# Attention scores from 64-row half heads in place of zero-padded queries, in both blocks

## The chip, the cores and the metric

The kernel runs on one core of a Trainium2 chip. The metric is the device time of one execution in microseconds; the median of the runs shown stands for a kernel. The profile is of one further execution.

## What is computed

Two transformer blocks follow each other on 256 tokens of width 1024, all in float32. Of the first block, what matters here is neighbourhood attention with 8 heads of 64:

```python
proj = jnp.einsum('bsd,de->bse', h, w_in[l])
q, k, v, a, g = jnp.split(proj, splits, axis=-1)
...
s = jnp.einsum('brcqhd,brckwhd->bhrcqkw', qg, kg,
               preferred_element_type=jnp.float32) * (Dh ** -0.5)
s = s + bias.astype(jnp.float32)[None]
s = jnp.where(col_mask[:, :, None, :], s, -jnp.inf)
p = jax.nn.softmax(s, axis=(-2, -1))
```

A convolution branch, an output projection and an expert layer (16 experts, width 2048) follow. The second block has differential attention: 16 score heads of 64 form 8 pairs, and the softmax of the second of a pair, times lambda, is taken from that of the first. There are 256 queries and 512 keys (256 of a context, 256 of the tokens); queries and keys are rotated (rope).

```python
q = axial_rope(q, rows, cols)
k = axial_rope(k, rows, cols)
...
s = jnp.einsum('bqhd,bkhd->bhqk', qblk, k).astype(jnp.float32) * (DIFF_DH ** -0.5)
a = jax.nn.softmax(s, axis=-1).reshape(B, DIFF_HEADS, 2, Q_BLK, Lk)
a = a[:, :, 0] - lam * a[:, :, 1]
```

After it come a gating branch, output projections, and a retrieval layer that gathers 16 rows for each token and each of 8 heads from a table in memory.

## The kernel before

Queries and keys lie transposed: the 128 partitions of a chunk hold the 64 features of one head and, below them, the 64 of the next, and tokens run along the free axis. A score product of one head would have 64 rows only. The kernel before makes it a product of 128 rows instead. It keeps the queries twice as wide, with an axis for the half: in half 0 the lower 64 partitions are zeros, in half 1 the upper ones. Both products of a chunk then read the whole key chunk, and the zeros take the other head out.

Block 1. The buffer is `qz` (L346), cleared by POOL (L347). `q_evac` (L386) copies the projected queries from PSUM with two ScalarE instructions per pair of chunks, one for each half. `head_pair` (L424) has one chunk: for both halves `hh` and both blocks of 128 queries `t` it multiplies (L430) into one PSUM bank for each half; then come bias and maximum on VectorE (L434, L436), exponentials and scaling on ScalarE, transposes (L452) and the product with the values (L461). The latter writes the two heads to the two halves of the partitions and so has the 128*64 form. Four such generators are advanced by hand, among the value projection (`proj_N`, L111), the convolution (VectorE L366, and TensorE L376 for the last chunk) and the matrix products of the modulation (`ada`, L270, 128*32 form).

Block 2. The buffer is `q2z` (L862), in the slot of a weight buffer; POOL clears the two unused quarters (L863, L864). `blk_T` projects (L93). `rope_evac` (L874) copies a chunk to `rr` on ScalarE (L879), shuffles it (L880), multiplies by sine on POOL (L881) and by cosine on VectorE (L882), and adds on VectorE (L884): for queries in two adds of 64 partitions, one for each half, for keys in one add of 128. `attend` (L896) is a generator for chunk `d` and query block `t`, 16 in all: two products (L901) into two PSUM banks, softmax on VectorE and ScalarE (L905 to L912), transposes (L916), copy (L918), product with the values (L922). The loop at L947 advances them in turn with `fill`, which holds the other projections of the block (L111, L93).

A projection takes its weights in two parts: ScalarE rounds (`wh`, L68), VectorE, or POOL for every fourth part in block 2, subtracts (`wl`, L75). Weights are loaded on SP's queue into a ring of buffers. The order of the instructions on an engine is in most of the program not that of the text: a planner lays it out when the program is built, by what is ready, with the text's order as priority; only behind L1061 is it held to the text. In the profile, for instance, some products of L376 stand between those of L270 and the transposes L279 that the text has right behind L270.

In the profile a float32 product shows as two records of weight load and two of product.

Of the kernel before, what the change touches and what calls it, by code (L numbers as in the profile page):

```python
# [5 lines left out]
F32 = mybir.dt.float32  # L6
# [3 lines left out]
AF = mybir.ActivationFunctionType  # L10
# [26 lines left out]
def body(tc, A, out, x1_in=None, dump=None, parts="1234"):  # L37
    nc = tc.nc
    mm = nc.tensor.matmul
    tt_ = nc.vector.tensor_tensor  # L40
    act = nc.scalar.activation
# [77 lines left out]
    def run(g):  # L119
        for _ in g:  # L120
            pass
# [103 lines left out]
    W = w_es.enter_context(pool(name="W", bufs=1, side="right"))  # L225
# [99 lines left out]
    if "1" in parts:  # L325
        p1 = ExitStack()
        P1 = p1.enter_context(pool(name="P1", bufs=1))
# [5 lines left out]
        hl = HP.tile([128, 2, 8, 256], F32R, name="h0", tag="h")  # L333
# [8 lines left out]
        def sl(c2):  # L342
            return slice(c2 * 2, c2 * 2 + 2)


        qz = P1.tile([128, 4, 2, 256], F32, name="qz", tag="qz")  # L346
        nc.gpsimd.memset(qz, 0.0)  # L347
        kT = P1.tile([128, 4, 256], F32, name="kT")
        vv = P1.tile([128, 2, 512], F32, name="vv")
        mp = [P1]  # L350
# [33 lines left out]
            next(cv)  # L384
        next(ad)
        def q_evac(c2, p):  # L386
            for hh in range(2):
                r = slice(hh * 64, hh * 64 + 64)
                act(qz[r, sl(c2), hh], p[r], AF.Copy)

        for _ in proj_T(P1, wload(A["w_in"][0]), hl, q_evac):
            pass
# [31 lines left out]
        def head_pair(hc):  # L424

            sp = []
            for hh in range(2):
                p = ps((128, 2, 256))
                for t in range(2):
                    mm(p[:, 1 - t], lhsT=qz[:, hc, hh, t * 128:(t + 1) * 128], rhs=kT[:, hc, :], start=True, stop=True)  # L430
                s = P1.tile([128, 2, 256], F32, name="s", tag="of", bufs=6)
                b = bias[:, hc * 2 + hh]
                b = bass.AP(tensor=b.tensor, offset=b.offset, ap=[b.ap[0], [128, 2], [1, 256]])
                nc.vector.scalar_tensor_tensor(out=s, in0=p, scalar=0.125, in1=b, op0=OP.mult, op1=OP.add)  # L434
                st = P1.tile([128, 6], F32, name="st", tag="st", bufs=4)
                nc.vector.tensor_reduce(out=st[:, 0:2], in_=s, axis=AX.X, op=OP.max, negate=True)  # L436
                sp.append((s, st))
            yield
            for s, st in sp:
                for t in range(2):  # L440
                    act(s[:, t], s[:, t], AF.Exp, bias=st[:, t:t + 1], accum_out=st[:, 2 + t:3 + t])
                nc.vector.reciprocal(out=st[:, 4:6], in_=st[:, 2:4])
            for s, st in sp:
                for t in range(2):
                    act(s[:, t], s[:, t], AF.Copy, scale=st[:, 4 + t:5 + t])
            yield
            at = []
            for s, st in sp:
                pt = pq((128, 2, 256))
                for kc in range(2):  # L450
                    for t in range(2):
                        nc.tensor.transpose(pt[:, kc, t * 128:(t + 1) * 128], s[:, 1 - t, kc * 128:(kc + 1) * 128], ident)  # L452
                aT = P1.tile([128, 2, 256], F32, name="aT", tag="of", bufs=6)
                act(aT, pt, AF.Copy)
                at.append(aT)
            yield
            po = pq((128, 256), name="po")
            for kc in range(2):
                for hh in range(2):
                    h = hc * 2 + hh  # L460
                    mm(po[hh * 64:hh * 64 + 64, :], lhsT=vv[:, kc, h * 64:(h + 1) * 64], rhs=at[hh][:, kc], start=kc == 0, stop=kc == 1)  # L461
            act(oT[:, hc], po, AF.Copy)
            yield
# [395 lines left out]
    nc.scalar.dma_start(out=x_dr, in_=X.rearrange("p t d -> p (t d)"))  # L859
    ga = XP.tile([128, 8, 256], F32, name="ga", tag="x")  # L860
    ring[:2] = [0, 3]
    qz = W.tile([128, 8, 2, 256], F32, name="q2z", tag="wa", bufs=1)  # L862
    nc.gpsimd.memset(qz[0:64, :, 1], 0.0)  # L863
    nc.gpsimd.memset(qz[64:128, :, 0], 0.0)  # L864
    zg2 = W.tile([128, 2, 8, 256], F32, name="zg2", tag="wb", bufs=1)
    zu, gs = zg2[:, 0], zg2[:, 1]

    def blk_T(src, x, evac):
        return proj_T(P3, wload(src), x, evac, pool_every=4)
# [4 lines left out]
    def rope_evac(dst_of):  # L874
        def f(c2, p):
            for c in range(2):
                raw = AT.tile([128, 256], F32, name="rr", tag="rr", bufs=2)
                sh = AT.tile([128, 256], F32, name="rs", tag="rs", bufs=2)
                act(raw, p[:, c], AF.Copy)  # L879
                nc.vector.stream_shuffle(sh, raw, [i ^ 16 for i in range(32)])  # L880
                nc.gpsimd.tensor_tensor(out=sh, in0=sh, in1=rope[:, 1], op=OP.mult)  # L881
                tt_(out=raw, in0=raw, in1=rope[:, 0], op=OP.mult)  # L882
                for r, d in dst_of(c2 * 2 + c):
                    tt_(out=d, in0=raw[r], in1=sh[r], op=OP.add)  # L884
        return f

    for b in range(2):
        run(blk_T(WI[b], hl, rope_evac(lambda c: [(slice(i * 64, i * 64 + 64), qz[i * 64:i * 64 + 64, b * 4 + c, i]) for i in range(2)])))
    for b in range(2):
        run(blk_T(WI[2 + b], hl, rope_evac(lambda c: [(slice(0, 128), kall[:, b * 4 + c, 256:512])])))  # L890
    for b in range(2):
# [4 lines left out]
    def attend(d, t):  # L896

        st = AT.tile([128, 8], F32, name="ast", tag="ast", bufs=3)
        pp = [ps(name="psc") for _ in range(2)]
        for i in range(2):  # L900
            mm(pp[i], lhsT=qz[:, d, i, t * 128:(t + 1) * 128], rhs=kall[:, d, :], start=True, stop=True)  # L901
        yield
        e = [None, None]
        for i in range(2):
            nc.vector.tensor_reduce(out=st[:, i:i + 1], in_=pp[i], axis=AX.X, op=OP.max)  # L905
            nc.vector.tensor_scalar(out=st[:, i:i + 1], in0=st[:, i:i + 1], scalar1=-0.125, scalar2=None, op0=OP.mult)
            e[i] = AT.tile([128, 512], F32, name="e%d" % i, tag="e%d" % i, bufs=2)
            act(e[i], pp[i], AF.Exp, bias=st[:, i:i + 1], scale=0.125, accum_out=st[:, 2 + i:3 + i])
        nc.vector.reciprocal(out=st[:, 4:6], in_=st[:, 2:4])
        tt_(out=st[:, 6:7], in0=st[:, 5:6], in1=lam, op=OP.mult)  # L910
        nc.vector.tensor_scalar(out=e[1], in0=e[1], scalar1=st[:, 6:7], scalar2=None, op0=OP.mult)
        nc.vector.scalar_tensor_tensor(out=e[0], in0=e[0], scalar=st[:, 4:5], in1=e[1], op0=OP.mult, op1=OP.subtract)  # L912
        yield
        pt = ps((128, 4, 128))
        for kc in range(4):
            nc.tensor.transpose(pt[:, kc], e[0][:, kc * 128:(kc + 1) * 128], ident)  # L916
        aT = AT.tile([128, 4, 128], F32, name="a2T", tag="a2T", bufs=2)
        act(aT, pt, AF.Copy)  # L918
        yield
        po = ps((128, 128))  # L920
        for kc in range(4):
            mm(po, lhsT=aT[:, kc], rhs=vall[:, kc, d * 128:(d + 1) * 128], start=kc == 0, stop=kc == 3)  # L922
        nc.vector.tensor_copy(out=oall[:, t, d * 128:(d + 1) * 128], in_=po)
        yield
# [591 lines left out]
```

## Time and profile before

| | |
|---|---|
| three runs | 2153.0, 2155.0, 2160.1 us |
| median | 2155.0 us |
| profiled execution, its own time | 2150.8 us |
| its span | 2148.1 us |
| TensorE busy | 1647.5 us (77%) |
| VectorE busy | 907.8 us (42%) |
| ScalarE busy | 494.0 us (23%) |
| POOL busy | 461.2 us (21%) |

By time: block 1 up to about 165 us, the experts to about 1130, block 2's projections to 1215, its attention to 1330, the rest of its mixing to about 1450, and the gathers up to the end. Busy shares of the whole span mix stages with different limits; each stage is read by itself. TensorE's clock has two levels, 2.4 GHz (granted share 1.00) and 1.2 GHz (0.50); a share between is a mean over a stretch. Records of products overlap in time, since each holds its own ending; the distance of their starts, not their length, is what one costs in a row of them.

### The profile page before, as it was taken

The page shows a single profiled execution, that of the slowest core. Times are in us where ns is not written, and L with a number is a line of the kernel's source. Part 1 is how long each engine was busy: PE and PEld are TensorE (multiplying, and loading weights), DVE is VectorE, ACT ScalarE, POOL GpSimd, SP SyncE. Part 2 cuts the span into 40 slices and gives each one's busy share as a digit, 9 for nine tenths or more (in the row PEclk, how much of TensorE's full clock was granted, in tenths as well). Part 3 has the DMA queues.
Part 4 walks back from the last instruction along what each step waited for, and adds up shares of the span by engine and source line. Part 5 has one row for each costly group of instructions (what it writes and reads, how often), then busy time and mean ns, then how long its engine had stood idle before and what let it go on. Part 6 is the DMA issues. An engine that isn't in the chain of part 4 may idle for free. (4 is left out here: it accounts for less than half of the span.)

```text
span 2148.1 us, 21498 instructions
## 1 busy us (share of the span) xinstructions
PE 1647.5 (77%) x8132; PEld 850.3 (40%) x8132; DVE 907.8 (42%) x1951; ACT 494.0 (23%) x985; POOL 461.2 (21%) x341
## 2 busy tenths in 40 slices
PE   7998758776766566666567999985987887888776
PEld 7754213321211111111117889975443433443332
DVE  5833110000000000000008866856977766776754
ACT  5652100000000000000005556542222222232121
POOL 0012000000000000000003311224555555554552
PEclk9998887888878888778879999996999999999999
DMA  8779999999999999999995523528999999999996
GB/s 359 286 275 373 427 425 420 420 428 422 416 428 425 428 427 426 427 426 427 428 425 197 186 90 126 208 89 323 406 420 421 421 421 421 421 422 421 421 421 263
DMA packets 81974, 784.90 MB, mean 365 GB/s; under 512 B 12752, under 2 KB 13136, under 8 KB 18640
## 3 DMA queue, kind: packets, MB, share of 16 engines
q1 hardware_dynamic: 39920, 508.25, 57.1%
q0 software_dynamic: 36864, 268.45, 30.1%
q10 hardware_dynamic: 5088, 6.84, 1.1%
q8 instruction: 64, 1.05, 0.2%
q14 instruction: 38, 0.31, 0.0%
HBM read 780.35 MB, written 3.16 MB: 365 GB/s over the span
## 5 line engine op out<-in xcount | busy, mean ns | idle before, releaser
L1333 PE MATMUL acc<-uv,dgu 128*128 128x512 f32 x1024 | 490.1, 635 | 122.8 <-ACT dgu L1331 122.6
L1307 POOL DMA_INDIRECT uv<-in_peer_uv_dram,ei x256 | 333.3, 1302 | 302.0 <-DMA uv<-in_peer_uv_dram,ei 153.1
L1315 DVE CUSTOM_DVE_ANT_0 uv<-uv,xn 128x1024 f32<-128x1024 f32 x256 | 313.3, 1224 | 150.1 <-DMA uv<-in_peer_uv_dram,ei 138.6
L1333 PEld LDWEIGHTS acc<-uv,dgu 128*128 128x128 f32 x1024 | 202.9, 203 | 380.7 <-issue 233.2
L714 PE MATMUL pd<-w,hidT 128*32 128x512 f32 x1024 | 177.7, 816 | 103.3 <-DMA w<-in_w_down_dram 96.6
L697 PE MATMUL pu<-w,xsT 128*32 128x512 f32 x1024 | 158.1, 746 | 97.9 <-DMA w<-in_w_up_dram 97.9
L697 PE MATMUL pg<-w,xsT 128*32 128x512 f32 x1024 | 156.7, 740 | 88.3 <-DMA w<-in_w_gate_dram 88.3
L703 DVE TENSOR_TENSOR hid<-pu,hid 128x512 f32<-128x512 f32 x16 | 11.0, 690 | 496.8 <-PE pu L697 465.8
L863 POOL MEMSET q2z<- 64x2048 f32 x1 | 1.8, 1797 | 860.2 <-PE pd L714 860.2
L93 PE MATMUL pp<-h,wh 128*128 128x256 f32 x896 | 168.9, 290 | 2.2 <-DVE h L82 1.3
L93 PEld LDWEIGHTS pp<-h,wh 128*128 128x128 f32 x896 | 142.4, 195 | 7.2 <-DVE h L82 1.9
L718 DVE COPY part<-pd 128x512 f32<-128x512 f32 x16 | 11.1, 692 | 289.9 <-PE pd L714 289.9
L93 PE MATMUL pp<-h,wl 128*128 128x256 f32 x448 | 128.6, 287 | 3.8 <-DVE wl L75 2.7
L714 PEld LDWEIGHTS pd<-w,hidT 128*32 128x32 f32 x1024 | 39.4, 132 | 224.4 <-DMA w<-in_w_down_dram 145.9
L68 ACT ACTIVATE wh<-w 128x1024 fp32r<-128x1024 f32 x99 | 104.2, 1058 | 95.4 <-PE pp L93 62.0
L697 PEld LDWEIGHTS pu<-w,xsT 128*32 128x32 f32 x1024 | 32.0, 124 | 221.3 <-DMA w<-in_w_up_dram 161.1
L75 DVE TENSOR_TENSOR wl<-w,wh 128x1024 fp32r<-128x1024 f32 x78 | 97.2, 1252 | 50.3 <-ACT wh L68 50.1
L1324 ACT ACTIVATE a<-dots 128x4 f32<-128x4 f32 (+1 forms) x66 | 13.5, 205 | 445.0 <-DVE dots L1315 445.0
L75 POOL TENSOR_TENSOR wl<-w,wh 128x1024 fp32r<-128x1024 f32 x22 | 55.8, 2537 | 276.8 <-ACT wh L68 276.4
L702 ACT ACTIVATE hid<-pg 128x512 f32<-128x512 f32 x16 | 9.6, 597 | 441.3 <-PE pg L697 441.2
L697 PEld LDWEIGHTS pg<-w,xsT 128*32 128x32 f32 x1024 | 30.5, 122 | 200.7 <-DMA w<-in_w_gate_dram 137.1
L1331 ACT ACTIVATE dgu<-cst,a 128x128 f32<-128x128 f32 x256 | 82.7, 391 | 34.7 <-DVE a L1326 27.6
(353 smaller groups left out, 2101.7 us busy)
## 6 DMA issues: line engine op xcount, KB each, us to landing
w<-in_w_up_dram SPq DMA_DIRECT2D x64, 2048.0 KB, 20.9
w<-in_w_gate_dram SPq DMA_DIRECT2D x64, 2048.0 KB, 21.2
w<-in_w_down_dram SPq DMA_DIRECT2D x63, 2048.0 KB, 21.4
w<-in_w_in_dram SPq DMA_DIRECT2D x22, 2048.0 KB, 9.0
w<-in_w_ada_dram SPq DMA_DIRECT2D x12, 2048.0 KB, 9.3
w<-in_w_out_dram SPq DMA_DIRECT2D x4, 2048.0 KB, 8.2
rw<-in_peer_w_query_dram SPq DMA_DIRECT2D x12, 512.0 KB, 8.3
w<-in_w_branch_attn_dram SPq DMA_DIRECT2D x2, 2048.0 KB, 7.9
```

The source lines that it names most:

```text
L68: i = act(wh, raw, AF.Copy) if he is None else he.tensor_copy(out=wh, in_=raw)
L75: i = eng.tensor_tensor(out=wl, in0=raw, in1=wh.bitcast(F32), op=OP.subtract)
L93: mm(pp[c // 2][:, c % 2], lhsT=wp[a][:, k2 * 512 + c * 128:k2 * 512 + (c + 1) * 128], rhs=hl[:, b, kd], start=kd == 0 and n == 0 and c % ...
L697: mm(p[j * 32:(j + 1) * 32, :], lhsT=xsT[:, kd, e * 32:(e + 1) * 32], rhs=w[:, k2 * 2048 + j * 512:k2 * 2048 + (j + 1) * 512], start=kd == ...
L703: tt_(out=hid, in0=pu, in1=hid, op=OP.mult)
L714: mm(pd[h][j * 32:(j + 1) * 32, :], lhsT=hidT[:, q, j * 32:(j + 1) * 32], rhs=w[:, j * 1024 + h * 512:j * 1024 + (h + 1) * 512], start=q = ...
L718: nc.vector.tensor_copy(out=part[:, 512:1024], in_=pd[1])
L1307: nc.gpsimd.indirect_dma_start(out=r, out_offset=None, in_=UV, in_offset=bass.IndirectOffsetOnAxis(ap=eis[u][:, k:k + 1], axis=0))
L1315: nc.vector.tensor_tensor_reduce(out=x, in0=x, in1=hx[:, u % 2], scale=1.0, scalar=0.0, op0=OP.mult, op1=OP.add, accum_out=dots[:, j:j + 1])
L1324: act(a[:, 0:n], dots[:, 0:n], AF.Gelu)
L1331: act(dg, ident, AF.Copy, scale=a[:, j:j + 1])
L1333: mm(acc[t][b], lhsT=dg, rhs=r[:, D + b * 512:D + (b + 1) * 512], start=h == 0 and k == 0, stop=h == 7 and k == 15)
```

## The change

The padded buffers become plain ones, half as large, in the same slots: `qT1` for `qz` and `q2` for `q2z`. The three memsets go. In block 1, `q_evac` copies both halves in one instruction; in block 2, the queries' add of the rope is one of 128 partitions, as for the keys. Each score product reads 64 partitions of the queries and the same 64 partitions of the keys. The products' count, order and targets stay.

```diff
-        qz = P1.tile([128, 4, 2, 256], F32, name="qz", tag="qz")
-        nc.gpsimd.memset(qz, 0.0)
+        qT1 = P1.tile([128, 4, 256], F32, name="qT1", tag="qz")
...
         def q_evac(c2, p):
-            for hh in range(2):
-                r = slice(hh * 64, hh * 64 + 64)
-                act(qz[r, sl(c2), hh], p[r], AF.Copy)
+            act(qT1[:, sl(c2)], p, AF.Copy)
...
                 for t in range(2):
-                    mm(p[:, 1 - t], lhsT=qz[:, hc, hh, t * 128:(t + 1) * 128], rhs=kT[:, hc, :], start=True, stop=True)
+                    mm(p[:, 1 - t], lhsT=qT1[hh * 64:hh * 64 + 64, hc, t * 128:(t + 1) * 128], rhs=kT[hh * 64:hh * 64 + 64, hc, :], start=True, stop=True)
...
-    qz = W.tile([128, 8, 2, 256], F32, name="q2z", tag="wa", bufs=1)
-    nc.gpsimd.memset(qz[0:64, :, 1], 0.0)
-    nc.gpsimd.memset(qz[64:128, :, 0], 0.0)
+    q2 = W.tile([128, 8, 256], F32, name="q2", tag="wa", bufs=1)
...
     for b in range(2):
-        run(blk_T(WI[b], hl, rope_evac(lambda c: [(slice(i * 64, i * 64 + 64), qz[i * 64:i * 64 + 64, b * 4 + c, i]) for i in range(2)])))
+        run(blk_T(WI[b], hl, rope_evac(lambda c: [(slice(0, 128), q2[:, b * 4 + c])])))
...
         for i in range(2):
-            mm(pp[i], lhsT=qz[:, d, i, t * 128:(t + 1) * 128], rhs=kall[:, d, :], start=True, stop=True)
+            mm(pp[i], lhsT=q2[i * 64:i * 64 + 64, d, t * 128:(t + 1) * 128], rhs=kall[i * 64:i * 64 + 64, d, :], start=True, stop=True)
```

## Rows read from the trace of the kernel before

**Rows 1.** The page, section 4: the chain that ended last, shares by line.

```profile
DMA uv<-in_peer_uv_dram,ei 21%; PE pp L93 5%; PE acc L1333 2%; DVE uv L1315 2%; PE pp L111 2%; PE psc L901 1%; PE pp L1084 1%; PE ps L922 1%; ACT dgu L1331 0%; PE pp L1191 0%; PE ps L916 0%; DVE wl L75 0%; POOL uv L1307 0%; POOL wl L75 0%; ACT wh L68 0%
```

**Rows 2.** Windows: stretch, length, busy us by PE PEld DVE ACT POOL, clock, DMA, GB/s.

```profile
72.00:90.00 18.00, 18.00 (x91) 13.78 (x91) 17.72 (x45) 10.43 (x26) 0.00 (x0) 1.00 0.71 255
...
300.00:1000.00 700.00, 459.64 (x2530) 132.39 (x2534) 46.48 (x68) 28.41 (x46) 0.00 (x0) 0.82 1.00 425
...
1290.00:1330.00 40.00, 39.97 (x288) 34.84 (x288) 26.01 (x54) 26.40 (x45) 5.26 (x2) 1.00 0.30 110
...
1500.00:2000.00 500.00, 419.77 (x1172) 206.67 (x1173) 365.80 (x939) 126.71 (x321) 263.94 (x202) 0.94 1.01 419
```

**Rows 3.** Score lines by source (ns min/median/max), then their first group in the timeline.

```profile
L901 PE MATMUL psc<-kall,q2z x64: 590/593/596, 1220.0 to 1325.3; 128*128 128x512 f32 x64
...
L430 PE MATMUL ps<-kT,qz x32: 377/379/484, 73.9 to 116.7; 128*128 128x256 f32 x32
...
1220.04 3.60 PE L901 MATMUL psc<-kall,q2z 128*128 128x512 f32 x8
```

**Rows 4.** Timeline of TensorE around column-tiled groups: start, us, line, form, count.

```profile
1117.34 1.95 PE L714 MATMUL pd<-w,hidT 128*32 128x512 f32 x16 [1.36 <-DMA w<-in_w_down_dram]
...
68.72 0.40 PE L93 MATMUL pp<-h,wh 128*128 128x256 f32 x2
68.97 0.28 PE L93 MATMUL pp<-h,wl 128*128 128x256 f32 x1
69.17 1.92 PE L270 MATMUL pa<-w,cT 128*32 128x512 f32 x16
71.03 0.73 PE L111 MATMUL pp<-wh,h 128*128 128x512 f32 x2
...
83.81 1.89 PE L430 MATMUL ps<-kT,qz 128*128 128x256 f32 x8
...
97.96 1.08 PE L461 MATMUL po<-aT,vv 128*64 128x256 f32 x8
98.97 2.00 PE L430 MATMUL ps<-kT,qz 128*128 128x256 f32 x8
```

**Rows 5.** Timeline, block 2's attention: last softmax step and transposes, two of 16.

```profile
1227.65 2.77 DVE L912 SCALAR_TENSOR_TENSOR e<-e,ast,e 128x512 f32<-128x512 f32 x1
...
1232.02 0.60 PE L916 MATMUL ps<-cst,e 128*128 128x128 f32 x4
...
1276.20 0.75 DVE L912 SCALAR_TENSOR_TENSOR e<-e,ast,e 128x512 f32<-128x512 f32 x1
...
1281.39 0.60 PE L916 MATMUL ps<-cst,e 128*128 128x128 f32 x4
```

**Rows 6.** Rope: source view of L884, timeline at 1160, window behind it.

```profile
L884 DVE TENSOR_TENSOR q2z<-rr,rs x16: 400/422/2635, 1160.3 to 1183.2; 64x256 f32<-64x256 f32 x16
L884 DVE TENSOR_TENSOR kall<-rr,rs x8: 410/414/2624, 1188.4 to 1206.9; 128x256 f32<-128x256 f32 x8
...
1160.28 3.95 DVE L884 TENSOR_TENSOR q2z<-rr,rs 64x256 f32<-64x256 f32 x4
1161.12 2.40 POOL L75 TENSOR_TENSOR wl<-w,wh 128x1024 fp32r<-128x1024 f32 x1 [1.05 <-ACT wh L68]
...
1164.61 1.22 DVE L75 TENSOR_TENSOR wl<-w,wh 128x1024 fp32r<-128x1024 f32 x1
...
1165.88 0.39 PE L93 MATMUL pp<-h,wl 128*128 128x256 f32 x1 [2.69 <-DVE wl L75]
...
1167.50:1170.00 2.50, 2.50 (x14) 2.50 (x13) 2.47 (x4) 0.41 (x1) 0.46 (x1) 0.50 0.80 328
```

**Rows 7.** Timeline of POOL: two of the three memsets, POOL's next work.

```profile
1.73 1.81 POOL L347 MEMSET qz<- 128x2048 f32 x1
...
1121.26 1.80 POOL L864 MEMSET q2z<- 64x2048 f32 x1
...
1131.95 2.50 POOL L745 TENSOR_TENSOR X<-X,fg 128x512 f32<-128x512 f32 x2 [8.90 <-ACT sj L744]
```

## Prediction

> **What bounds the kernel now.** I read the page's chain of waits first, then windows by stage, then the score products by source line, then single timelines. The chain ends in a long run of row gathers, and ahead of it mostly in TensorE work; the two projection lines and the second block's score line each hold a piece [rows 1]. The windows say who is busy where. From 300 to 1000 us (experts) and from 1500 to 2000 us (the gathers) the DMA engines are full (share 1.00 and 1.01), so the lengths of these two stages are fixed and only their start can move. Both attention stages are another matter: in block 2, from 1290 to 1330, TensorE is busy 39.97 of 40 us at full clock, VectorE 26.01, ScalarE 26.40, and DMA has a share of 0.30. In block 1, 72 to 90, TensorE is busy 18.00 of 18 us, but VectorE 17.72 as well [rows 2]. So a microsecond less of TensorE work in block 2's attention should be a microsecond of the end, because the first gather waits for everything in between; in block 1 VectorE stands close behind.
>
> **The change, part by part.**
>
> *Score products, block 2.* Each float32 product leaves two records, and the records follow each other in one queue: eight take 3.60 us with 0.593 for the last, so (3.60 - 0.593) / 7 = 0.43 us a record [rows 3]. 64 records are 27.5 us, 1.72 per attend step (four records). Half of the rows that they multiply are zeros. With 64 rows each, products 0 and 1 of a step use different halves of the array and write different banks, so they can run side by side: 0.86 per step instead of 1.72.
>
> No product of before uses half of the rows, so the gain is bounded from column tiles, the nearest rows. Sixteen records of the 32-column form of the down projection take 1.95 us; in one queue they would take 16 x 0.43 = 6.9 us. Four run side by side, four times 0.43 plus 0.16 of ending latency. The 64-column products of L461 do the same two by two: eight records in 1.08 us, against 1.89 us for eight of the same 256 columns at full width [rows 4]. I take full overlap; the other end, none, is the first rival.
>
> The price is the change of array shape, because the work around every step is 128*128. Column tiles show it. Two full-width records of 0.28 us last 0.40 together, so they start 0.12 apart; behind the one at 68.97 the next is due at 69.09, but the 32-column group starts at 69.17: 0.08 late. The next line starts at 71.03, 1.86 us behind the group's start, of which 4 x 0.43 = 1.72 are products: 0.14 more. Behind the 64-column group the eight records of L430 last 2.00 where they last 1.89 elsewhere: 0.11 more. In and out together 0.33. The 64-column group itself gives 98.97 - 97.96 = 1.01 against 4 x 0.216 = 0.86 (0.216 being (1.89 - 0.379) / 7), so 0.15, and with the same 0.08 and 0.11 the pair is 0.34 [rows 3, 4]. Row tiles have twice to four times the weight columns of these, so I take 0.35 and hold 0.2 and 0.5 as bounds. The first two steps are neighbours, so there are 15 pairs of changes: 16 x 0.86 - 15 x 0.35 = 8.5 us (bounds 6.3 and 10.8).
>
> The Trainium skill, TensorEngine Tiling (Array Packing), section Tiling Modes, speaks against the change here: a change of the mode, though not of the tile within one, drains TensorE. The trace agrees, with 0.33 and 0.34 us per pair on column tiles. The same skill, TensorE: Matmul & The Clock Gate, Part 3, gives 3.07 times for four 32-row tiles; if two tiles reached 3.07 / 4 of their ideal, a step would hold 1.12 instead of 0.86 us of products and the term would be an estimated 4.3 us instead of 8.5.
>
> *What comes up next there.* VectorE's softmax starts on product 0, which still takes two records, so it starts no earlier, while the transposes that need it come about 0.5 us earlier for each shortened step ahead of them, so at most 1.0. For an ordinary step the softmax ends at 1276.20 + 0.75 and the transposes start at 1281.39, 4.4 us of cover. The tight early one ends at 1227.65 + 2.77 = 1230.42 for transposes at 1232.02: 1.6 us [rows 5]. So the cover holds, and I take off 0.5 us for the few tight places: 8.0.
>
> *Rope of the queries.* Sixteen 64-row adds of 0.422 us become eight 128-row adds; the keys' adds, of that form, have a median of 0.414 [rows 6]. That is 3.4 us of VectorE. Most of it lies beside TensorE's projection, but at one place it does not: four of these adds start at 1160.28 and take 3.95 us together, because POOL's 2.40 us subtraction starts at 1161.12 and the third add waits beside it. VectorE's own subtraction for the next weights starts only at 1164.61, and TensorE stands idle for 2.69 us until 1165.88. Behind this idle time the granted clock is 0.50 (1.2 GHz) from 1167.5 to 1170, which costs 2.5 x 0.50 = 1.25 us at least [rows 6]. With two adds instead of four, VectorE is done at about 1160.28 + 2 x 0.42 = 1161.12, just as POOL starts. If POOL goes first again, the subtraction starts when POOL ends (1163.52) and after a shuffle of some 0.4: about 1163.9 instead of 1164.61, gain 0.7. If VectorE goes first, stall and slow clock both go: 2.69 + 1.25 = 3.9. I take 1.5, nearer the first because the two engines meet at the same instant and a part of the stall has other reasons; bounds 0 and 3.9.
>
> *Score products, block 1.* Four head pairs of eight records: 1.72 becomes 0.86 us, so 3.4. Fewer changes of shape are new, since three of the groups already border on tiled work [rows 4]: one full pair, two halves, one none, about 0.7, so 2.7 us of TensorE. Both halves of a head pair write banks of their own. But VectorE has 0.28 us of slack in 18 [rows 2] while the convolution lasts, which covers the first two groups, so only the later ones are likely to count: 1.3 us, bounds 0 and 2.7. The end of block 1 starts the experts, and what it gains starts their full DMA flow earlier.
>
> *Edits with one answer.* The three memsets (1.81 us, and two of 1.80) go. The first stands on POOL at 1.73, 70 us ahead of the first score product [rows 3]; the last ends at 1123.06, before POOL's next work at 1131.95. They gain nothing, and their length would count only if POOL were the last there [rows 7]. Two of four ScalarE copies of block 1's queries go, beside a full TensorE: nothing. The buffers keep their places in the same slots, so no load starts at another point.
>
> **Sum.** 8.0 + 1.5 + 1.3 = 10.8 us off the profiled execution's 2150.8 us (span 2148.1): 2140.0. That execution lies 4.2 us below the median of the three runs, 2155.0, and the shift is the same there: 2144.2 us.
>
> **Rivals.**
>
> *Row tiles run one after the other (slower).* If the array takes one row half at a time, each product keeps its 0.43 us per record, and the changes of shape are pure cost: 15 x 0.35 + 0.7 = 6.0 us. If the change from one half to the other drains as well, at half of a pair, 20 x 0.18 = 3.6 more. With the rope's 1.5 us gained: +8.1, so 2163 us. It decides where overlap saves less than 0.35 of the 0.86 us, that is under 41%. For it: no row here shows row tiles. Against it: column tiles overlap nearly fully, within the same two-record scheme [rows 4].
>
> *The two records of a product stay in order across the tiles.* If records start strictly as they are written, product 1 can start only beside the second record of product 0: three slots of 0.43 instead of two. A step gains 0.43 - 0.35 = 0.08; all of them 15 x 0.08 + 0.43 = 1.6 us, block 1 nothing, and with the rope 3.1: 2152. Against it: the eight records of L461 are written as pairs of records too, and (1.08 - 0.38) / 0.216 = 3.2 steps behind the first start make them four slots, not five [rows 3, 4]. The Trainium skill, TensorE: Matmul & The Clock Gate, Part 3, states this rule: matmuls start and end in program order. By that a step would be the 1.29 us used here; the trace does not bear it out for column tiles, unless the records are already interleaved in the program.
>
> *Another engine or another order eats it.* The order of instructions on each engine follows what is ready, and with eight VectorE and two ScalarE instructions gone it can turn out differently; or VectorE (26 of 40 us) becomes last in the tight steps. If half of the block 2 term goes that way and the rest is lost: about -4, 2151.
>
> **How the numbers follow.** About 0.3%, 6.5 us, is what a measurement of this kernel can tell from no change. Forecast 0.66; serial row tiles 0.11; records in order 0.11; eaten 0.12. The forecast's own range comes from its bounds: 6.3 + 0 + 0 less 0.5 gives 2149, and 10.8 + 3.9 + 2.7 gives 2138. The range reaches to the two middle rivals and the run-to-run spread above 2155 (the slowest of three is 2160): 2136 to 2157, which leaves out the slower rival and a little at the low end. Faster by over 0.3%: the forecast but for its weak end, 0.64, and a little of the eaten case, together 0.66. Slower: most of the serial rival, 0.09. Within: 0.25.
>
> **What would show it.** In the profile after, 64-row forms of the score records whose pairs start within hundredths of a microsecond, steps of 1.2 us where there were 1.72, and TensorE still without idle time from 1215 on; attention there some 8 us shorter. A step of 1.7 us or more is the serial rival; 1.6 is the one with records in order. Idle time of TensorE behind VectorE's L912 or L75 is the third. The stall at 1163 shows the rope's term. I would be wrong above all if row tiles do not overlap, or if the shift of the attention's end does not reach the first gather.

## The result, and the profile after

| | before | after |
|---|---|---|
| median of the runs, us | 2155.0 (2152.55 to 2160.13) | 2143.26 (2139.38 to 2148.23) |
| profiled execution, us | 2150.77 (span 2148.1) | 2139.38 (span 2137.5) |
| first score product of block 1, us | 73.88 | 72.68 |
| first expert product, us | 188.07 | 186.56 |
| end of the experts' last product, us | 1129.27 | 1128.91 |
| first rope add of the queries, us | 1160.28 | 1159.97 |
| first score product of block 2, us | 1220.04 | 1214.70 |
| last product with V in block 2 ends, us | 1337.21 | 1326.25 |
| first gather issued, us | 1467.24 | 1456.41 |

After / before is 0.9945, 95% interval [0.9923, 0.9966]: about 11.9 us faster (7 to 17). 2144.2 was forecast. In the two profiles after leads by 1.2 us ahead of block 1, 1.5 us at the first expert product, 0.3 us at the rope, 5.3 us at block 2's first score product, 11.0 us at the end of its attention, and 10.8 us at the first gather. So two stages carry nearly all of it: 5.0 us between the first rope add and the first score product, and 5.6 us in block 2's attention.

The page's chain of waits, section 4, shares by line, as in [rows 1]. The score line has gone from 1% to 0%, and VectorE's and POOL's weight subtractions (L75) stand at 1% and 0%.

```profile
DMA uv<-in_peer_uv_dram,ei 20%; PE pp L93 4%; PE acc L1327 3%; DVE uv L1309 2%; PE pp L111 1%; PE pp L1185 1%; PE pp L1078 1%; DVE wl L75 1%; PE ps L916 0%; PE psc L895 0%; ACT dgu L1325 0%; POOL uv L1301 0%; ACT wh L68 0%; POOL wl L75 0%; PE ps L910 0%
```

Windows of after (stretch, length, busy us by PE, PEld, DVE, ACT and POOL, clock, DMA share, GB/s), to be held against [rows 2].

```profile
72.00:90.00 18.00, 17.20 (x92) 12.21 (x91) 17.50 (x45) 11.61 (x31) 0.00 (x0) 1.00 0.78 295
300.00:1000.00 700.00, 461.18 (x2526) 132.03 (x2522) 46.47 (x68) 28.41 (x46) 0.00 (x0) 0.82 1.00 424
...
1290.00:1326.00 36.00, 35.11 (x268) 31.13 (x267) 24.04 (x47) 24.90 (x43) 5.28 (x2) 1.00 0.32 118
1500.00:2000.00 500.00, 421.67 (x1176) 206.89 (x1175) 364.45 (x932) 128.19 (x324) 265.33 (x204) 0.95 1.01 420
```

Experts and gathers are as full of DMA as before. In both attention stages TensorE is no longer full: 17.20 of 18 us in block 1, 35.11 of 36 in block 2, where it was 18.00 of 18 and 39.97 of 40.

The score records by source line (ns min/median/max), to be held against [rows 3].

```profile
L895 PE MATMUL psc<-kall,q x64: 588/590/694, 1214.7 to 1314.2; 64*128 64x512 f32 x64
...
L426 PE MATMUL ps<-kT,qT x32: 375/377/481, 72.7 to 114.2; 64*128 64x256 f32 x32
```

A 64-row record lasts 0.590 us where the full one lasted 0.593: what became shorter is not the record but the step. TensorE's timeline in after (start, us, line, form, count, idle before):

```profile
1214.39 0.39 PE L111 MATMUL pp<-wl,h 128*128 128x512 f32 x1
1214.70 1.99 PE L895 MATMUL psc<-kall,q 64*128 64x512 f32 x8
1216.62 0.73 PE L111 MATMUL pp<-wh,h 128*128 128x512 f32 x2
...
1223.95 1.13 PE L895 MATMUL psc<-kall,q 64*128 64x512 f32 x4
1225.15 0.63 PE L910 MATMUL ps<-cst,e 128*128 128x128 f32 x4
...
1230.92 0.63 PE L910 MATMUL ps<-cst,e 128*128 128x128 f32 x4 [0.46 <-DVE e L906]
...
1303.54 1.80 PE L895 MATMUL psc<-kall,q 64*128 64x512 f32 x4
...
1312.60 1.16 PE L916 MATMUL ps<-vall,a2T 128*128 128x128 f32 x8 [0.89 <-ACT a2T L912]
```

Eight records in 1.99 us are four places of 0.43 with the entry and the ending, not eight; four in 1.13 us are two. The two row halves work side by side. The other rows are where the gain leaks: two idle times, and at 1303.54 one pair that needs 1.80 us instead of 1.13.

The rope in after, VectorE, POOL and the window behind, to be held against [rows 6]:

```profile
1159.97 0.75 DVE L878 TENSOR_TENSOR q<-rr,rs 128x256 f32<-128x256 f32 x2
1160.64 1.22 DVE L75 TENSOR_TENSOR wl<-w,wh 128x1024 fp32r<-128x1024 f32 x1
...
1160.82 3.31 POOL L75 TENSOR_TENSOR wl<-w,wh 128x1024 fp32r<-128x1024 f32 x1 [1.05 <-ACT wh L68]
...
1165.00:1172.50 7.50, 7.50 (x65) 7.50 (x64) 7.50 (x14) 3.66 (x7) 2.51 (x4) 1.00 0.76 282
```

VectorE's two adds are done before POOL starts, its subtraction follows at once, and now POOL's lasts longer (3.31 us, 2.40 before). The clock stays at its full level. In before the same window, and TensorE's waits from 1157 to 1220 (line, waited for, us in total, times, longest), were:

```profile
1165.00:1172.50 7.50, 6.62 (x42) 6.62 (x43) 7.08 (x13) 2.31 (x4) 2.16 (x2) 0.77 0.76 280
...
PE pp L93 <- DVE wl L75: 2.7, 1, 2.7
PE pp L93 <- POOL wl L75: 1.1, 1, 1.1
PE pp L111 <- POOL wl L75: 0.3, 1, 0.3
```

and TensorE's waits in after, from 1157 to 1214:

```profile
PE pp L93 <- POOL wl L75: 0.4, 1, 0.4
PE pp L111 <- POOL wl L75: 0.2, 1, 0.2
```

4.1 us of waits became 0.6, and the clock of 0.77 over 7.5 us was another 1.7: together 5.2, against 5.0 measured between the marks.

Between block 1 and the experts a lead is lost. The lead of after is 3.8 us at the router's running sum (L647 before, L643 after) and 1.5 at the first expert product. Before, VectorE and then POOL:

```profile
182.11 0.68 DVE L647 TENSOR_TENSOR_SCAN cs<-on,sel 16x256 f32<-16x256 f32 x1
182.82 0.41 DVE L648 TENSOR_TENSOR cs<-cs,sel 16x256 f32<-16x256 f32 x1
...
182.86 2.60 POOL L633 TENSOR_TENSOR xs<-xn,xs 128x1024 fp32r<-128x1024 f32 x1 [1.26 <-ACT xn L632]
```

After:

```profile
178.28 0.68 DVE L643 TENSOR_TENSOR_SCAN cs<-on,sel 16x256 f32<-16x256 f32 x1
178.99 2.57 DVE L644 TENSOR_TENSOR cs<-cs,sel 16x256 f32<-16x256 f32 x1
...
178.94 2.34 POOL L629 TENSOR_TENSOR xs<-xn,xs 128x1024 fp32r<-128x1024 f32 x1 [1.26 <-ACT xn L628]
```

The same small product takes 0.41 us when it starts 0.04 us ahead of POOL's subtraction, and 2.57 us when it starts 0.05 us behind it. The router's transposes, and with them the gather of tokens for the first expert, wait for it.

### The profile page after: what moved, and what is told of

The parts are those of the page before. It is cut to its first block, busy times and chain, and to the rows that moved or that the text cites. A ratio compares the mean times of both kernels' runs of the same rounds, so it can differ in the third digit from the quotient of the medians.

```text
span 2137.5 us, 21483 instructions
## 1 busy us (share of the span) xinstructions
PE 1637.5 (77%) x8132; PEld 839.1 (39%) x8132; DVE 905.8 (42%) x1943; ACT 491.9 (23%) x983; POOL 454.9 (21%) x338
## 5 line engine op out<-in xcount | busy, mean ns | idle before, releaser
L693 PE MATMUL pu<-w,xsT 128*32 128x512 f32 x1024 | 164.6, 774 | 105.1 <-DMA w<-in_w_up_dram 105.1
L693 PE MATMUL pg<-w,xsT 128*32 128x512 f32 x1024 | 150.4, 713 | 84.5 <-DMA w<-in_w_gate_dram 84.5
L75 DVE TENSOR_TENSOR wl<-w,wh 128x1024 fp32r<-128x1024 f32 x78 | 98.1, 1265 | 46.8 <-ACT wh L68 46.7
L75 POOL TENSOR_TENSOR wl<-w,wh 128x1024 fp32r<-128x1024 f32 x22 | 57.1, 2595 | 269.9 <-ACT wh L68 269.6
```

The source lines that it names most:

```text
L75: i = eng.tensor_tensor(out=wl, in0=raw, in1=wh.bitcast(F32), op=OP.subtract)
L693: mm(p[j * 32:(j + 1) * 32, :], lhsT=xsT[:, kd, e * 32:(e + 1) * 32], rhs=w[:, k2 * 2048 + j * 512:k2 * 2048 + (j + 1) * 512], start=kd == ...
```

## Experiments

Eleven kernels. The first four take the change apart; the others test what ate a part of the gain. Ratios are against the kernel before; each is an estimate with its 95% interval and can differ a little from the quotient of two medians. "Attention" is the stage from block 2's first score product to the last product with V: 739 TensorE records in each kernel for which a window is shown here.

**Block 2's scores alone** (the rope's adds stay two of 64 partitions, block 1 as before):

```diff
-    qz = W.tile([128, 8, 2, 256], F32, name="q2z", tag="wa", bufs=1)
+    q2 = W.tile([128, 8, 256], F32, name="q2", tag="wa", bufs=1)
...
-            mm(pp[i], lhsT=qz[:, d, i, t * 128:(t + 1) * 128], rhs=kall[:, d, :], start=True, stop=True)
+            mm(pp[i], lhsT=q2[i * 64:i * 64 + 64, d, t * 128:(t + 1) * 128], rhs=kall[i * 64:i * 64 + 64, d, :], start=True, stop=True)
```

> Of the change only the score products of block 2: they read 64 rows of a plain query buffer, and the rope still writes the queries in two adds of 64 partitions; block 1 as before. My theory, that the parts act by themselves: the stall of 2.7 us at 1163 us and the slow clock behind it stay as before, steps of four score records go from 1.72 to 1.2 us, and the attention of block 2 (first score product to the last product with the values, 117.2 us before, 111.6 after) takes about 111.5 us, so 5.5 to 6.5 us off the end: about 2149. Rival, that the rope's merged adds are what makes room for the softmax in the attention: the attention keeps about 117 us here.

Measured: 2150.01 us, ratio 0.9978 [0.9967, 0.9989], and the attention is as long as in after (111.54 and 111.55). So the attention's 5.6 us come from the score products, and owe nothing to the rope. In the whole time 0.22% is 4.7 us, a little under the 5.5 to 6.5 expected. The profile shows less, a first gather only 0.4 us earlier than before's: this execution reaches the rope 2.6 us later (the router's race, below, and longer experts), and 2.5 us more pass between the attention's end and the first gather. The window over the attention, in before, after and this kernel:

```profile
1220.04:1337.21 117.17, 117.14 (x739) 97.03 (x738) 78.23 (x164) 71.19 (x127) 15.02 (x6) 1.00 0.31 115
```

```profile
1214.70:1326.25 111.55, 110.03 (x739) 91.15 (x739) 78.39 (x164) 70.63 (x127) 15.39 (x6) 1.00 0.32 121
```

```profile
1222.77:1334.31 111.54, 110.04 (x739) 91.08 (x739) 78.36 (x164) 70.66 (x127) 15.40 (x6) 1.00 0.33 121
```

**The rope's add alone** (one add of 128 partitions into a plain buffer; products of all 128 rows):

```diff
-        run(blk_T(WI[b], hl, rope_evac(lambda c: [(slice(i * 64, i * 64 + 64), qz[i * 64:i * 64 + 64, b * 4 + c, i]) for i in range(2)])))
+        run(blk_T(WI[b], hl, rope_evac(lambda c: [(slice(0, 128), q2[:, b * 4 + c])])))
...
+            mm(pp[i], lhsT=q2[:, d, t * 128:(t + 1) * 128], rhs=kall[:, d, :], start=True, stop=True)
```

> Of the change only block 2's plain query buffer: one add of 128 partitions per chunk and no memsets. Block 1 as before. Left out: the separation of the two heads of a pair, since the products of block 2 read all 128 rows of queries and keys and so sum both heads; their number, size and time are those of before. My theory: VectorE reaches its subtraction ahead of POOL's, the stall of 2.7 us and the 3.4 us at 1.2 GHz behind it are gone, the first score product comes 5 us earlier against the start of the rope, the attention takes its 117 us as before, and the end moves by about -5: 2150. Rival, that the stall went because the whole schedule stood 0.3 us earlier in that run, by chance: no more than 1 us.

Measured: 2149.8 us, ratio 0.9974 [0.9959, 0.9989]. From the rope's first add to the first score product 54.65 us, where before had 59.76: the 5 us expected. From the end of the experts' last product it is 86.34 us instead of 90.77; attention 117.19, as before. TensorE's waits from 1160 to 1222 hold no wait for VectorE's subtraction any more:

```profile
PE pp L93 <- POOL wl L75: 0.4, 1, 0.4
PE pp L111 <- POOL wl L75: 0.3, 1, 0.3
```

The merged add by itself is worth 4.4 to 5.1 us up to the first score product, and in the whole time about as much as the score products (0.26% and 0.22%).

**Block 1 alone:**

```diff
-            for hh in range(2):
-                r = slice(hh * 64, hh * 64 + 64)
-                act(qz[r, sl(c2), hh], p[r], AF.Copy)
+            act(qT1[:, sl(c2)], p, AF.Copy)
...
-                    mm(p[:, 1 - t], lhsT=qz[:, hc, hh, t * 128:(t + 1) * 128], rhs=kT[:, hc, :], start=True, stop=True)
+                    mm(p[:, 1 - t], lhsT=qT1[hh * 64:hh * 64 + 64, hc, t * 128:(t + 1) * 128], rhs=kT[hh * 64:hh * 64 + 64, hc, :], start=True, stop=True)
```

> Of the change only block 1; block 2 as before. In the profile after, block 1's lead against before was 3.9 us at the router's product, of which 1.2 were there ahead of the first changed instruction, and 2.2 were lost again at one VectorE multiplication that started 0.05 us behind a POOL subtraction and waited for it. My theory: the lead at the router's product is 2 to 4 us, and at the end of the experts 0 to 1.5, with the time at 2153 to 2156. Rival, that the experts' full DMA queue takes any lead: there would be a lead behind the router too, and none at the end of the experts.

Measured: 2154.06 us, ratio 1.0001 [0.999, 1.0011]. No difference. At the end of the router product it leads before by 1.8 us, a little under the 2 to 4 expected; the router's small product lost its race here too, so the first expert product comes at 188.67 us, 0.60 later than before, and the experts end 2.5 us later, where 0 to 1.5 earlier was expected. The three parts add up to -0.22, -0.26 and +0.01%, together -0.47%; the whole change has -0.55 [-0.77, -0.34].

**Both products on the same row half** (the change, but product 1 reads the same 64 rows as product 0):

```diff
-            mm(pp[i], lhsT=q2[i * 64:i * 64 + 64, d, t * 128:(t + 1) * 128], rhs=kall[i * 64:i * 64 + 64, d, :], start=True, stop=True)
+            mm(pp[i], lhsT=q2[0:64, d, t * 128:(t + 1) * 128], rhs=kall[0:64, d, :], start=True, stop=True)
```

> The changed kernel, with both products of a step of block 2's attention reading the lower 64 rows, so that they cannot run beside each other. Left out: the scores of the second head of each pair (the first head's take their place). My theory, that the whole gain is overlap and a product of 64 rows costs what one of 128 rows does: records start 0.43 us apart, a step with its two changes of shape takes 1.72 plus 0.36 us, and the attention is about 16 x 0.86 = 13.8 us longer than after, less up to 2.4 us of waits for the softmax that go away: 122.5 to 125 us, total 2154 to 2157. Rival, that fewer rows are cheaper by themselves: steps stay near 1.2 us, total near 2143.

Measured: 2150.67 us, ratio 0.9995 [0.9985, 1.0006]; attention 122.28. The window over it, and a step in the timeline:

```profile
1215.63:1337.91 122.28, 122.28 (x739) 96.77 (x739) 76.19 (x164) 71.54 (x127) 15.09 (x6) 1.00 0.30 111
...
1226.34 1.98 PE L895 MATMUL psc<-kall,q 64*128 64x512 f32 x4
```

Four records take 1.98 us, against 1.13 with two halves. Fewer rows alone save nothing; the whole gain is the overlap. And with TensorE full here (122.28 of 122.28) and no overlap, what the stage has more than before is the price of the changes of shape alone: 122.28 - 117.17 = 5.1 us, for 15 pairs 0.34 each (0.36 against 116.88, the kernel before without POOL's subtractions, below). The attention lies just under the 122.5 to 125 us expected, the median below the 2154 to 2157. The Trainium skill, TensorEngine Tiling (Array Packing), section Tiling Modes, says that a change of the mode drains TensorE; the trace fits this, with 0.34 us for in and out together, though the draining itself is in no row.

**What ate the rest of the attention's gain: all weight subtractions beside it on VectorE** (the change; POOL otherwise takes every fourth):

```diff
+    every = [4]
...
-        return proj_T(P3, wload(src), x, evac, pool_every=4)
+        return proj_T(P3, wload(src), x, evac, pool_every=every[0])
...
+    every[0] = 0
     fl = fill()
...
     run(fl)
+    every[0] = 4
```

> The changed kernel, with all weight subtractions that run beside block 2's attention on VectorE, where every fourth was on POOL. In the changed kernel the attention takes 111.6 us; 16 shortened steps (13.8 us) less 15 pairs of shape changes at 0.36 (5.4 us) would have given 108.8, and the rest is waits for the softmax. My theory, that VectorE is held up beside POOL's 2.5 us subtractions (single instructions of 2.8 and 3.1 us in place of 0.75 and 1.22): these go, and the attention takes 109 to 110.5 us, total 2141 to 2143. Rival, that VectorE simply has too much to do in the shorter steps: the added 1.22 us each make it longer, 112 to 114 us.

Measured: 2140.02 us, ratio 0.9931 [0.9916, 0.9946]; attention 109.42, 2.1 us shorter than after, although VectorE has more to do. The window, and TensorE's longest wait in the stage:

```profile
1217.08:1326.50 109.42, 109.06 (x739) 90.81 (x739) 79.72 (x170) 70.44 (x127) 0.00 (x0) 1.00 0.33 123
...
PE ps L918 <- ACT a2T L914: 0.3, 1, 0.3
```

VectorE needs 79.72 us of it instead of 78.39, TensorE idles 0.36 us instead of 1.52, and works 109.06 us instead of 110.03; 0.67 us of this difference is the pair at 1303.54, which overlaps again (1.13 us instead of 1.80). In after, the way of the harm is visible: VectorE's L906 at 1222.23 took 2.77 us beside POOL's subtraction of 1222.06, which pushed the next subtraction to 1224.92 and the next step's softmax behind it; TensorE's idle time at 1230.92 is the end of this chain.

```profile
1222.06 2.39 POOL L75 TENSOR_TENSOR wl<-w,wh 128x1024 fp32r<-128x1024 f32 x1 [12.10 <-ACT wh L68]
...
1222.23 2.77 DVE L906 SCALAR_TENSOR_TENSOR e<-e,ast,e 128x512 f32<-128x512 f32 x1
...
1224.92 1.21 DVE L75 TENSOR_TENSOR wl<-w,wh 128x1024 fp32r<-128x1024 f32 x1
1226.06 0.28 DVE L917 COPY oall<-ps 128x128 f32<-128x128 f32 x1
1226.26 1.27 DVE L899 TENSOR_REDUCE ast<-psc 128x1 f32<-128x512 f32 x2
...
1230.02 0.75 DVE L906 SCALAR_TENSOR_TENSOR e<-e,ast,e 128x512 f32<-128x512 f32 x1
```

**The same edit in the kernel before**, as the counter-test:

> The kernel before with the weight subtractions of the projections beside block 2's attention all on VectorE, none on POOL. Theory (before, TensorE is full in that stage and VectorE only follows; VectorE's waits beside POOL's subtractions came to the end of a step only after the scores were shortened): the stage from the first score product to the last product with V keeps its 117.2 us, within 0.3. Rival (POOL's subtractions held the stage back already in the kernel before, and what freeing VectorE gains has nothing to do with the shorter scores): 115 to 116 us, as far below before as the same edit is below the changed kernel (2.1).

Measured (one execution): attention 116.88, 0.3 us less than before's 117.17, with TensorE busy for all of it:

```profile
1220.73:1337.61 116.88, 116.88 (x739) 96.93 (x738) 80.24 (x170) 71.37 (x128) 0.00 (x0) 1.00 0.31 116
```

So VectorE's waits beside POOL cost the kernel before 0.3 us, where they cost the changed kernel 2.1: the change made them count. With both kernels freed of them, the score products are worth 116.88 - 109.42 = 7.5 us.

**The rope's stall: the queries' weight subtractions on VectorE, in the kernel before** (`every[0] = 0` around the first projection loop alone):

> The kernel before, with the weight subtractions of the two query projections of block 2 all on VectorE, so that POOL has none of 2.4 us there. My theory, that the stall at 1163 us came from VectorE waiting beside POOL and not from the number of adds: the four adds of 64 partitions take about 1.7 us together in place of 3.95, the stall of TensorE shrinks to under 1 us, the clock stays at 2.4 GHz, and the first score product comes 3 to 5 us earlier against the first add. Rival, that the number of adds is what counts: the stall stays near 2.7 us, or grows by the added subtraction.

Measured: 2146.62 us, ratio 0.9974 [0.9958, 0.999]; the profiled execution was the longest of seven (2158.2). From the end of the experts to the first score product 87.47 us instead of 90.77. From the first add the stage is nearly unchanged (59.05 and 59.76): the add itself comes earlier behind the experts, 28.42 us instead of 31.01, so the number that was given for that mark did not come out, the one for the whole did. Four 64-row adds without POOL's subtraction beside them (POOL's multiplication for the rope still runs, until 1165.56), and TensorE's waits for VectorE from 1160 to 1222:

```profile
1164.88 2.27 DVE L886 TENSOR_TENSOR q2z<-rr,rs 64x256 f32<-64x256 f32 x4
...
PE pp L93 <- DVE wl L75: 1.6, 2, 0.9
```

The adds take 2.27 us where they took 3.95 [rows 6]; a later group of four, at 1178.49, has no POOL instruction beside it and takes 1.73, the time expected. The longest wait is 0.9 us, not 2.69, and the granted clock stays at 1.00 from 1165 to 1172.5. POOL's subtraction beside VectorE made the long stall. The two waits that are left come to 1.6 us. VectorE now also has the subtractions that POOL had, and it still meets POOL's multiplications for the rope; which of these makes the 1.6 us is not settled.

**The race at the router** (the change, with POOL's second subtraction made to wait for VectorE's small product):

```diff
-                nc.gpsimd.tensor_tensor(out=xs[:, 1, t], in0=xn2, in1=xs[:, 0, t].bitcast(F32), op=OP.subtract)
+                low = nc.gpsimd.tensor_tensor(out=xs[:, 1, t], in0=xn2, in1=xs[:, 0, t].bitcast(F32), op=OP.subtract)
...
-            tt_(out=cs, in0=cs, in1=sel, op=OP.mult)
+            after(low, tt_(out=cs, in0=cs, in1=sel, op=OP.mult))
```

> The changed kernel, with POOL's second subtraction of the router's stage (L629) made to wait for VectorE's multiplication L644, which in the changed kernel starts 0.05 us behind it and then takes 2.57 us in place of 0.41. My theory: the multiplication takes 0.4 us again and the first expert product comes 2.1 us earlier against the router's product; since the experts are bound by DMA whose queue fills from there, the whole lead reaches the end: about -2 against after, 2141. Rival, that the DMA queue of the experts runs ahead on its own: the lead is there at the first expert and gone at the last, and the time is that of after, 2143.

Measured: 2140.94 us, ratio 0.9938 [0.9922, 0.9954]. From the end of the router product to the first expert product 12.42 us, where after had 14.82 and before 12.41:

```profile
180.62 0.41 DVE L644 TENSOR_TENSOR cs<-cs,sel 16x256 f32<-16x256 f32 x1
...
181.17 2.36 POOL L629 TENSOR_TENSOR xs<-xn,xs 128x1024 fp32r<-128x1024 f32 x1 [1.83 <-DVE cs L644]
```

The 2.4 us are this one race. At the end of the experts the kernel leads after by 0.9 us (1128.02 and 1128.91), but the experts' length varies by more than that: 941 to 946 us among the profiles here. What the race is worth in the whole time isn't settled by this.

**The same wait without and with block 1's change**, to see block 1 without the race:

> The kernel before with POOL's second subtraction for the router made to wait for VectorE's product of running sum and selection, so that the race between the two always ends one way. Theory (the race alone sets the 2.4 us between router product and first expert product): 12.4 to 12.7 us from the end of the router product to the first expert product; first score product of block 1 to first expert product 114 us. The whole kernel: 0 to 2.4 us faster, depending on how often the kernel before loses the race by itself. Rival (another wait takes its place without the change): 14.8 us there.

> The score products of block 1 changed alone, with POOL's second subtraction for the router made to wait in the same way; to be held against the kernel before with the same wait. Theory (block 1's shorter scores reach the first expert product once the race is settled): first score product of block 1 to first expert product 0.2 to 2.7 us shorter than there, near 1.5, and up to 1.5 us in the whole time. Rival (the gain of block 1 is lost again before the router, to VectorE and the convolution): no difference at the first expert product beyond 0.3 us.

Measured: the wait alone 2151.91 us, ratio 0.9997 [0.9987, 1.0006], router to experts 12.68 us; with block 1's change 2149.26 us, ratio 0.9981 [0.9971, 0.999], 12.68 us. From the first score product to the first expert product 114.38 and 113.90 us: block 1 reaches the experts with 0.5 us. The timed ratios differ by 0.16%, 3.4 us, more than the profiles show, and block 1 alone without the wait had nothing. So block 1 is worth between nothing and some 3 us, and which isn't settled. Its stage varies: from the first score product to the end of the router product, seven profiles with the new block 1 have 98.9 to 101.4 us, six with the old one 101.3 to 101.9.

**Both improvements on the change** (the wait at the router, and the subtractions beside the attention on VectorE):

> The two edits of the runs before this one together, on the changed kernel. If both do what I think, -2 and -1.5 against after: about 2139.5. If neither reaches the end, 2143.

Measured: 2136.68 us, ratio 0.9919 [0.9903, 0.9934], the fastest of all here; attention 109.37, router to experts 12.68. Its interval overlaps that of the change (0.9923 to 0.9966) a little, so the gain over the change is likely rather than certain in the time; in the stage it is plain.

## Why the prediction was right, and where its terms were not

The forecast of 10.8 us off met 10.6 in the span. That it came so close is luck: none of the three terms had its size, and their errors cancel. 8.0, 1.5 and 1.3 were forecast; 5.6, 5.0 and 0.4 at the end of the experts were found.

*Overlap of row tiles.* Right, and fully: 1.13 us for four records, against 1.98 on one half. The rivals with serial tiles and with records in order fall: the first is what the kernel with one half does (attention +5.1 us), and the second would need three places, 1.29 us and the ending, where the four records last 1.13 in all. The estimate from four 32-row tiles, 1.12 us of products in a step, did not come out either: the 1.13 hold the ending as well. The first two records of a step begin together, and where product 1 had to wait for its bank, both records of product 0 had begun before it:

```profile
1214.70 0.70 PE L895 MATMUL psc<-kall,q 64*128 64x512 f32 x2
...
1303.54 1.12 PE L895 MATMUL psc<-kall,q 64*128 64x512 f32 x2
```

Two records in 0.70 us are side by side, two in 1.12 one behind the other. The Trainium skill, TensorE: Matmul & The Clock Gate, Part 3, has matmuls start in program order; taken by whole products, no row here speaks against it. What the first row rules out is the rival's reading by records, with three places in a step. How the records of two products stand in the program is in no row, so this stays open.

*Price of the shape changes.* Right: 0.35 taken from column tiles, 0.34 to 0.36 measured for row tiles (5.1 to 5.4 us in 15 pairs). (One sum on the way is a little off: four times 0.43 plus 0.16 makes 1.88 us, where the row of the down projection has 1.95 [rows 4]. The term does not hang on it.) So 13.8 - 5.1 = 8.7 would have been the stage's gain if nothing else came last.

*"So the cover holds, and I take off 0.5 us."* This step failed. 8.7 us were there for TensorE and 5.6 came out. The prediction looked at the softmax's lead in before [rows 5] and took the softmax as fixed. But its tightest row, the 2.77 us of L912 at 1227.65, was not a property of softmax: it was POOL's subtraction beside it, in before at 1227.48, and such a meeting delays all that VectorE does next. With 0.5 us less of TensorE per step, that delay reached TensorE: 0.46 and 0.89 us of idle time (of the latter 0.3 us stay without POOL's subtractions, so not all of it is theirs), and one pair without overlap. That one at 1303.54 is a bank: its second product waited for ScalarE's exponential of the step before (L902), itself late behind VectorE's subtraction of 3.10 us at 1298.99, which met POOL's. The first row is of before, the others of after, the last of them from its waits (us in total, times, longest):

```profile
1227.48 2.39 POOL L75 TENSOR_TENSOR wl<-w,wh 128x1024 fp32r<-128x1024 f32 x1 [12.10 <-ACT wh L68]
...
1298.15 2.86 POOL L75 TENSOR_TENSOR wl<-w,wh 128x1024 fp32r<-128x1024 f32 x1 [19.25 <-ACT wh L68]
...
1298.99 3.10 DVE L75 TENSOR_TENSOR wl<-w,wh 128x1024 fp32r<-128x1024 f32 x1
...
PEld psc L895 <- ACT e L902: 0.4, 1, 0.4
```

Without POOL's subtractions the same kernel gains 7.5 to 7.8 us, close to the 8.0. This is a small form of the rival "another engine eats it": 2.1 of the 3.1 us that are missing. Of the other 1.0 us, 0.4 is idle time that TensorE still has there; the rest is not settled.

*The rope.* The mechanism and both ends were right, the choice between them was wrong: "nearer the first because the two engines meet at the same instant". 0.7 was the price if POOL goes first, 3.9 if VectorE does. VectorE went first, at 1160.64 against 1160.82. This was not chance: from the first add to the first score product the six profiles with one add per chunk have 54.7 us, the seven with two 59.0 to 59.9. The rest up to 5.0 lies in a second wait for POOL's subtraction, 1.1 us in before and 0.4 in after, and in the slow clock, 1.7 us over its whole stretch where I had counted 1.25 for the window shown. Two adds saved 0.8 us of VectorE's time, and five of the end: what counts is who is first, and a value between two outcomes is the one that will not be seen.

*Block 1.* 1.3 us were counted. "The end of block 1 starts the experts" held, but between them stands the router, with a race that the prediction did not look at. In the profile of before VectorE won it by 0.04 us; in after it lost. Of five profiles of the old block 1 without the forced wait two won it, of four of the new one none. So a single profile can fall either way; whether the change tilts the race isn't settled. The shown lead of 3.8 us holds 1.2 us that was there before block 1's first score product, too.

*Edits with one answer.* For memsets and ScalarE copies "nothing" was forecast; no row speaks against it, and no run has them alone. *The end of the attention reaches the first gather*: in this pair, 11.0 us there and 10.8 at the gather. The stage between the two lasted 129.1 to 133.5 us among the thirteen profiles, with a granted clock of 0.96 in the shortest and 0.91 in the longest, so in a single profile some of a lead can be hidden there.

```profile
L1307 POOL DMA_INDIRECT uv<-in_peer_uv_dram,ei x256: 934/1285/1972, 1467.2 to 2112.7; - x128
```

```profile
L1301 POOL DMA_INDIRECT uv<-in_peer_uv_dram,ei x256: 936/1286/1992, 1456.4 to 2102.4; - x128
```

Before and after: first and last gather move together, so what is gained ahead of them is kept.

## What to carry to other kernels

Zero-padding a product to fill the array is to be checked against two real products on the two row halves: it is the overlap that pays, half of the two products' time less the change of shape, so neighbours of the same shape are worth arranging. Where an engine is full and another follows closely, a cover read in the old profile shrinks by each shortened step: look up what made the tightest step tight, since a collision of two other engines can be moved away. And where two engines start within 0.1 or 0.2 us of each other, price both outcomes and give each its chance instead of a value in between; the same order may come out every time, as at the rope, or not, as at the router.

## What the runs showed of the hardware that was not expected

In the meetings shown here VectorE and POOL hold each other up in element-wise work with two inputs, and the one that starts first wins: VectorE's product of 16x256 took 0.41 us started 0.04 us ahead of POOL's subtraction, and 2.57 us started 0.05 us behind it, while that subtraction took 2.34 us; when VectorE starts first, POOL's subtraction of 128x1024 lasts 3.31 us instead of 2.40. The Trainium skill, SBUF — State Buffer, section SBUF: two separate sides, states such a lock between VectorE's instructions with two inputs in SBUF and POOL's that read there, held by the first for its whole instruction; the trace agrees in both directions, with the 2.57 and the 3.31 us. A helper engine can thus cost the helped one nearly as much as it does: with POOL's six subtractions moved to VectorE, VectorE's busy time in the stage grew by 1.3 us only (78.39 to 79.72), although each takes 1.22 us there, 7.3 us in all.

The two halves of the array work side by side in float32 even though each product leaves two records (1.13 us for two products, 1.98 on one half); a product that has to wait for its bank lost the overlap for the whole pair (1.80 us instead of 1.13; the kernel with block 2's scores alone has the same at the same step, at 1311.60).
